# A two-layer decoder trunk on one core: row sums, maximum broadcast, gates and head norm of its mLSTM mixer, done in another way

## The chip, the cores and the metric

The kernel runs on one core of a Trainium2 chip. The engines of the core run side by side and meet through semaphores: PE (TensorE, matrix products, results into PSUM), DVE (VectorE), ACT (ScalarE), POOL (GpSimd), and SP, which issues DMAs. PEld is the loading of the stationary operand, which can overlap PE. The metric is device time in microseconds (us) of one execution. The kernel before was run three times: 999.59 us is the median, 999.35 the lowest, 1000.89 the highest.

## What is computed

A trunk of two layers over 256 tokens of width 1024, in fp32. Each layer has a SwiGLU block, a mixer, a second SwiGLU block and a gated input embedding, each between RMS norms. Layer 0 mixes with an mLSTM in four heads (keys of 128, values of 256), layer 1 with differential attention over keys and values that are shared. The change is in the mLSTM. Cut to what matters:

```python
def step(carry, inp):                       # reference: chunks of 128 tokens
    C, n, m = carry
    b = jnp.cumsum(lf, axis=-1)
    d = b[..., :, None] - b[..., None, :] + li[..., None, :]
    d = jnp.where(causal, d, -jnp.inf)
    inter = b + m[..., None]
    m_t = jnp.maximum(inter, jnp.max(d, axis=-1))
    w = jnp.exp(d - m_t[..., None])
    qk = jnp.einsum('bhtd,bhsd->bhts', qj, kj) * w
    num = jnp.einsum('bhts,bhsv->bhtv', qk, vj) + ...
    den = jnp.sum(qk, axis=-1) + ...
    h = num / jnp.maximum(jnp.abs(den), jnp.exp(-m_t))[..., None]
...
h = mlstm_chunkwise(q, k, v, log_i, log_f)   # log_i, log_f from x @ w_in[:, gates] + b_gates
h = rms_norm(h, head_norm[:, None, :])
return (jax.nn.sigmoid(o) * h) @ w_out
```

So per head and token there is a weighted sum of values (num), the sum of the weights themselves (den), a division, and an RMS norm over the 256 values of the head.

## The kernel before

**Numbers in parts.** A product of the trunk's weights is done as three fast products: each operand is split into a rounded high part and a remainder (`split`: ACT copies into an fp32r tile, DVE subtracts), and `mm3` (L507) adds high·high, high·low and low·high. An fp32r matmul is one pass of PE; a plain fp32 matmul is two rows in the profile. Weight tiles come as 128x2048 into `wraw` buffers, and become `whi` and `wlo`.

**The order is planned.** The program notes every operation first (`Notes.add`). `Notes.play` (L267) then lays them out with a cost model: per engine it takes, among the operations that can start, mostly the one of lowest rank, which is the order of the program text. For PE a change of operand kind adds a penalty; `kind` (L205) calls transposes "t", everything with an fp32r operand "r", and other matmuls by the size of their stationary operand. Plain fp32 matmuls and transposes are held back until their inputs have been there for a margin; those on one PSUM tile go together. Buffers of a pool are given in order of first use: ten `wraw`, eight `att` (128x512), three each of `sg`, `hh` and `hl`, and in PSUM three banks `accI`, four banks `accO`, one bank `tr`. Since `issue` calls all operations from one place, all stand on L433 in the profile, and one tells them apart by tile names.

**The mixer** is `mlstm` (L996), between about 185 and 285 us. The 256 tokens are two blocks of 128, t = 0 and 1.

- *Queries and keys*: per block two 512-wide products, each evacuated by `transposed` (L986): ACT copies with the norm's factor, PE transposes four 128x128 pieces, DVE copies them to `qT` or `kT`. `transposed` also serves the shared keys and the queries of layer 1, those with a factor.
- *Gates*: `pg` (L1035) has the eight gate rows, spread over 36, along partitions and the tokens along columns, in fp32; `pr` (L1036) spreads the norm's factor over 36 rows by a matmul with the identity. ACT copies `pr`, DVE multiplies. Then biases, log-sigmoid (ACT: exp and ln), a cumulative sum and a running maximum M by scans, all on four rows.
- *Values*: `block_pair` (L718), seven products of a Strassen scheme in place of eight, from `forms` of the inputs (`att` buffers). It ends with `use`; here that is `value`, which ACT does.
- *Heads* (`head`, L1067): PE spreads M's row of this head over 128 partitions (`pm`) and makes the scores (`pS`, fp32); DVE makes the argument of the exponential and, after ACT's exp, the weights `pTh`.
- *Outputs* (`outputs`, L1101): per block, PE makes `pd`, the sums of the weights, by matmuls with a column of ones, and `num`, two heads to a bank; DVE, ACT (squares) and POOL (power of −1/2) make the norm's factor, and DVE scales `num` by it into `hn`.
- *Output gate*: a second `block_pair` makes the gate's inputs and calls `opened` (L1156), which calls `outputs` and `gated`; `gated` multiplies and transposes.
- *Output product*: `proj` (L970) for each block, into two `accO` banks, and `post`.

The rank of the second `block_pair`'s last piece, and what hangs on it:

```python
        use(1, 1, z5)                                   # outputs(1)
        times(ax, quarter(1, 4), wt4, True)             # twelve matmuls
        if not end:
            use(1, 0, u2)                               # gated(0, 1)
        use(0, 1, ax)                                   # gated(1, 0), gated(1, 1)
```

and where the banks are asked for:

```python
        num = acc_out()                                 # two accO banks, for block t
        nums = [num[h // 2][:, h % 2 * DV:(h % 2 + 1) * DV] for h in range(HA)]
```

Of the kernel before, what the change touches and what calls it, by code (L numbers as in the profile page):

```python
# [16 lines left out]
P = 128  # L17
D = 1024
# [417 lines left out]
def trunk(nc, a):  # L436
    def T(shape, tag, bufs, dt=F32):
        return nc.tile("sb", shape, tag, bufs, dt)
# [4 lines left out]
    def acc_out():  # L443
        return [PT("accO", 512, 4) for _ in range(2)]
# [4 lines left out]
    def trp():  # L449
        return PT("tr", 512, 1)  # L450
# [4 lines left out]
    def piece():  # L455
        return T([P, 512], "att", ATT)
# [20 lines left out]
    def pair(*shape):  # L477
        b = T([P, 2, *shape], "wraw", NRAW)
        return [b[:, i] for i in range(2)]
# [506 lines left out]
    def transposed(pi, r, dst, t, c=1.0):  # L986
        q = piece()
        nc.scalar.activation(q, pi, AF.Copy, scale=r)
        pv = transpose4(q, 0)
        if c == 1.0:  # L990
            nc.vector.tensor_copy(dst[:, :, t * P:(t + 1) * P], pv)
        else:
            nc.vector.tensor_scalar(dst[:, :, t * P:(t + 1) * P], pv, c, None, op0=ALU.mult)


    def mlstm(l, xts, rs, raws, epilogue):  # L996
# [9 lines left out]
            out=mask_a[:, :P], in_=mask_a[:, :P], compare_op=ALU.is_ge, fill=BIG,  # L1006
            base=0, pattern=[[1, P]], channel_multiplier=-1,
        )
        ones = T([P, S], "sg", NSG)
        nc.gpsimd.memset(ones, 1.0)  # L1010

        wg = T([P, KD, 8], "att", ATT)
        nc.sync.dma_start(wg, a["mlstm_gates"])
# [14 lines left out]
        for t in range(NT):  # L1028
            tc_ = slice(t * P, (t + 1) * P)
            for b in range(2):  # L1030
                pi = acc_in()
                in_block(pi, xts[t], ws[b])
                transposed(pi, rs[t], qkT[b], t)
            for k in range(KD):
                nc.tensor.matmul(pg[:36, tc_], w36[:, k, :], raws[t][:, k, :], start=k == 0, stop=k == KD - 1)  # L1035
            nc.tensor.matmul(pr[:36, tc_], rs[t].to_broadcast([P, 36]), ident, start=True, stop=True)  # L1036
        rb = T([36, S], "att", ATT)
        nc.scalar.activation(rb, pr[:36, :S], AF.Copy)
        g36 = T([36, S], "att", ATT)
        nc.vector.tensor_tensor(g36, pg[:36, :S], rb, op=ALU.mult)  # L1040
        li = T([HA, S], "att", ATT)
        nc.vector.tensor_scalar(li, g36[0:HA, :], bg[:, 0:1], None, op0=ALU.add)
        z = T([HA, S], "att", ATT)
        nc.vector.tensor_copy(z, g36[32:36, :])
        nc.vector.tensor_scalar(z, z, bg[:, 1:2], None, op0=ALU.add)

        en = T([HA, S], "att", ATT)
        nc.vector.scalar_tensor_tensor(en, z, -1.0, z, op0=ALU.mult, op1=ALU.max)
# [4 lines left out]
        B = T([HA, S], "att", ATT)  # L1053
        nc.vector.tensor_tensor_scan(B, ones[:HA, :], z, 0.0, op0=ALU.mult, op1=ALU.add)
        nc.vector.tensor_tensor(li, li, B, op=ALU.subtract)
        M = T([HA, S], "sg", NSG)
        nc.vector.tensor_tensor_scan(M, li, li, -3.0e38, op0=ALU.max, op1=ALU.max)
        nc.vector.tensor_tensor(B, B, M, op=ALU.add)


        v = pair(D)
        pTs = []

        def value(b, t, src):
            nc.scalar.activation(v[t][:, b * 512:(b + 1) * 512], src, AF.Copy, scale=rs[t])

        def head(h):  # L1067
            pm, pS = acc_out()
            nc.tensor.matmul(pm[:, :S], ident[:HA, h:h + 1].to_broadcast([HA, P]), M, start=True, stop=True)
            arg = T([P, 384], "att", ATT)  # L1070
            nc.vector.scalar_tensor_tensor(
                arg[:, :S], pm[:, :S], at[:, h:h + 1], mask_a, op0=ALU.subtract, op1=ALU.max)
# [26 lines left out]
        room = pair(D)  # L1099

        def outputs(t):  # L1101
            num = acc_out()
            pd = trp()
            parts = [(slice(0, P), 0)] if t == 0 else [(slice(P, S), 0), (slice(S, 384), 1)]
            nums = [num[h // 2][:, h % 2 * DV:(h % 2 + 1) * DV] for h in range(HA)]
# [4 lines left out]
            for h in range(HA):  # L1110
                for i, (c, st) in enumerate(parts):
                    nc.tensor.matmul(nums[h], pTs[h][:, c], v[st][:, h * DV:(h + 1) * DV],
                                     start=i == 0, stop=i == len(parts) - 1)
            den = small(4)
            nc.vector.tensor_copy(den, pd[:, 0:4])
            nden = small(4)
            nc.vector.tensor_scalar(nden, den, -1.0, None, op0=ALU.mult)
            ad = small(4)
            nc.vector.tensor_tensor(ad, den, nden, op=ALU.max)
            mx = small(4)  # L1120
            nc.vector.tensor_tensor(mx, ad, enm[:, t * HA:(t + 1) * HA], op=ALU.max)
            c = small(4)
            nc.vector.reciprocal(c, mx)
# [4 lines left out]
            c2 = small(4)  # L1128
            nc.vector.tensor_tensor(c2, c, c, op=ALU.mult)
            vv = small(4)  # L1130
            nc.vector.tensor_tensor(vv, c2, sq, op=ALU.mult)
            ve = small(4)
            nc.vector.tensor_scalar(ve, vv, EPS, None, op0=ALU.add)
            rh = rpow(ve, 4)
            cr = small(4)
            nc.vector.tensor_tensor(cr, c, rh, op=ALU.mult)
            hn = room[t]
            for h in range(HA):
                cc = slice(h * DV, (h + 1) * DV)
# [362 lines left out]
```

## Time and profile before

| what | value |
|---|---|
| median of three runs | 999.59 us |
| span of the profiled execution (the page gives no other time of it) | 998.2 us |
| granted clock of PE, mean | 0.998 |
| mixer, 185 to 285 us: PE busy | 99.67 us |
| mixer: DVE busy | 94.19 us |
| mixer: ACT busy | 72.41 us |
| mixer: POOL busy | 14.06 us |

The profile is one execution, taken by the hardware profiler. Busy time counts an engine's instructions; matmuls are pipelined, so their durations overlap, and the distance between two starts tells what one costs. A row of the timeline has the start, the length, engine, line, operation, the tile written and the tiles read, the shape (for a matmul first the stationary operand's, rows*columns), and how many like it were merged.

### The profile page before, as it was taken

The numbers are of one execution on the slowest core, as the hardware profiler recorded it, in microseconds if no ns is written. First come the engines' busy times: TensorE is split into PE (matmuls) and PEld (weight loads), VectorE is DVE, ScalarE is ACT, GpSimd is POOL, SyncE is SP. The second block draws the span as 40 slices with busy tenths as digits, with TensorE's granted clock in tenths as the row PEclk, the third lists the DMA queues.
The fourth block names the chain that finished last, engine by engine and source line by source line (L and its number), as shares of the span: only waits on it lengthen the run. The fifth ranks groups of instructions, "written<-read, shape, count | busy, mean of one in ns | idle before, by whom it ended". The sixth has DMA issues, their size and how long they took to land.

```text
span 998.2 us, 12473 instructions
## 1 busy us (share of the span) xinstructions
PE 987.7 (99%) x4660; PEld 808.9 (81%) x4660; DVE 869.7 (87%) x897; ACT 688.6 (69%) x914; POOL 86.0 (9%) x122
## 2 busy tenths in 40 slices
PE   8999999999999999999999999999999999999997
PEld 7888888888888888888878888888888888888886
DVE  6977999799999799997799999898984988999883
ACT  7747777568856677776777767686775756776663
POOL 0010000300131000001120000000001200000010
PEclk9999999999999999999999999999999999999999
DMA  9999948766699989674699999964755999895511
GB/s 346 420 339 342 309 176 304 242 207 205 252 345 338 287 298 277 247 284 170 257 298 333 322 355 348 340 227 179 253 211 193 298 305 281 317 262 240 222 66 60
DMA packets 44995, 268.39 MB, mean 269 GB/s; under 512 B 5384, under 2 KB 5768, under 8 KB 16008
## 3 DMA queue, kind: packets, MB, share of 16 engines
q1 hardware_dynamic: 39464, 229.59, 60.0%
q0 software_dynamic: 5184, 37.75, 18.5%
q8 instruction: 36, 0.59, 0.2%
q10 hardware_dynamic: 288, 0.27, 0.1%
q14 instruction: 23, 0.19, 0.1%
HBM read 257.11 MB, written 10.49 MB: 268 GB/s over the span
## 4 chain that ended last, share of the span: by engine, by line
PE 48%; issue 2%; ACT 2%; POOL 1%; DVE 1%; POOLq 0%; DVEq 0%; ACTq 0%
PE accI L433 30%; PE accO L433 15%; PE tr L433 2%; POOL sm L433 1%; ACT sg L433 1%; DVE wlo_0r L433 0%; ACT wraw L433 0%; ACT whi_4r L433 0%; ACT whi_0r L433 0%; ACT att L433 0%; DVE wraw L433 0%; DVE xl_5r L433 0%; DVEq L1498 0%; ACT xh_3r L433 0%; POOLq L1498 0%
## 5 line engine op out<-in xcount | busy, mean ns | idle before, releaser
L433 DVE TENSOR_TENSOR wraw<-wraw,wraw 128x2048 f32<-128x2048 f32 x36 | 82.3, 2285 | 0.2
L433 ACT ACTIVATE whi_2r<-wraw 128x2048 fp32r<-128x2048 f32 (+1 forms) x47 | 75.7, 1619 | 8.8 <-PE accI L433 4.2
L433 ACT ACTIVATE whi_3r<-wraw 128x2048 fp32r<-128x2048 f32 (+1 forms) x46 | 75.6, 1651 | 8.1 <-PE accI L433 3.3
L433 ACT ACTIVATE whi_1r<-wraw 128x2048 fp32r<-128x2048 f32 (+2 forms) x48 | 72.5, 1522 | 12.4 <-PE accI L433 4.0
L433 ACT ACTIVATE whi_0r<-wraw 128x2048 fp32r<-128x2048 f32 (+2 forms) x47 | 72.6, 1550 | 10.2 <-PE accI L433 4.7
L433 ACT ACTIVATE whi_4r<-wraw 128x2048 fp32r<-128x2048 f32 (+1 forms) x45 | 73.5, 1647 | 8.4 <-DVE wraw L433 4.5
L433 ACT ACTIVATE whi_5r<-wraw 128x2048 fp32r<-128x2048 f32 (+1 forms) x47 | 74.0, 1587 | 6.2 <-PE accI L433 4.7
L433 ACT ACTIVATE att<-accI 128x512 f32<-128x512 f32 x72 | 42.9, 596 | 30.2 <-PE accI L433 30.2
L433 POOL DMA_DIRECT2D wraw<-in_ffn_in x32 | 28.5, 891 | 322.0 <-DMA wraw<-in_ffn_in 286.6
L433 POOL TENSOR_SCALAR sm<-sm 128x1 f32<-128x1 f32 x32 | 18.8, 587 | 331.7 <-ACT sg L433 331.7
L433 ACT ACTIVATE sg<-accI,sm 128x256 f32<-128x256 f32 x40 | 18.9, 473 | 32.0 <-PE accI L433 26.9
L433 ACT ACTIVATE sg<-att,sm 128x256 f32<-128x256 f32 x48 | 24.0, 505 | 23.9 <-DVE att L433 23.9
L433 POOL TENSOR_TENSOR sm<-sm,mhalf 128x1 f32<-128x1 f32 (+2 forms) x40 | 30.1, 753 | 113.4 <-DVE sm L433 110.8
L433 ACT ACTIVATE sg<-accO 128x512 bf16<-128x512 f32 (+2 forms) x46 | 20.1, 442 | 22.1 <-PE accO L433 20.0
L433 PEld LDWEIGHTS tr<-ident,sg 128*128 128x128 f32 x176 | 23.0, 140 | 14.4 <-DVE hl_0r L433 2.0
L433 PE MATMUL tr<-ident,sg 128*128 128x128 f32 x176 | 34.1, 275 | 0.0
L433 DVE SCALAR_TENSOR_TENSOR wraw<-wraw,sm,wraw 128x512 f32<-128x512 f32 x32 | 22.6, 749 | 12.3 <-POOL sm L433 12.3
L433 DVE TENSOR_TENSOR att<-accI,att 128x512 f32<-128x512 f32 x36 | 24.7, 687 | 7.7 <-PE accI L433 7.2
L433 DVE SCALAR_TENSOR_TENSOR sg<-accI,sm,sg 128x256 f32<-128x256 f32 x40 | 19.2, 480 | 12.1 <-ACT sg L433 11.9
L433 ACT ACTIVATE att<-accI,sm 128x512 f32<-128x512 f32 (+1 forms) x22 | 14.8, 671 | 20.9 <-PE accI L433 20.9
L433 ACT ACTIVATE sg<-wraw 128x512 bf16<-128x512 f32 x32 | 20.1, 629 | 13.1 <-DVE wraw L433 9.6
L433 DVE SCALAR_TENSOR_TENSOR sg<-att,sm,sg 128x256 f32<-128x256 f32 x48 | 22.9, 481 | 3.4 <-ACT sg L433 3.2
(608 smaller groups left out, 3252.2 us busy)
## 6 DMA issues: line engine op xcount, KB each, us to landing
wraw<-in_ffn_in SPq DMA_DIRECT2D x100, 1024.0 KB, 9.2
wraw<-in_ffn_out SPq DMA_DIRECT2D x44, 1024.0 KB, 7.7
wraw<-in_ffn_in POOLq DMA_DIRECT2D x32, 1024.0 KB, 13.7
wraw<-in_mlstm_in SPq DMA_DIRECT2D x14, 1024.0 KB, 5.1
wraw<-in_ple_gate SPq DMA_DIRECT2D x8, 1024.0 KB, 6.2
wraw<-in_w_kv SPq DMA_DIRECT2D x8, 1024.0 KB, 4.8
home<-wraw SPq DMA_DIRECT2D x28, 256.0 KB, 3.9
wraw<-home SPq DMA_DIRECT2D x14, 512.0 KB, 3.9
```

The lines of the kernel that those rows point to most:

```text
L433: getattr(getattr(self.nc, eng), name)(*args, **kw)
```

## The change

- `transposed`: the second copy, out of PSUM, is ACT's instead of DVE's, with the factor in it.
- Gates: the tokens are along partitions: `raws` is the stationary operand, the 36-wide weights move. ACT scales the result by the norm's factor, PE transposes it into `pr`, and the bias additions read `pr` from PSUM. The separate product, the copy of `z` and the matmul that spread the factor go.
- Maximum: M is held as two fp32r parts, on rows 0 to 3 and 32 to 35 of a tile of 36 rows (`mhl`, an `hh` buffer); `pick` (an `hl` buffer) has the identity's columns twice. `pm` is a single fp32r matmul of the two, with 36 rows. M lies in an `att` buffer instead of an `sg` buffer, and `ones` is four rows instead of 128.
- Values: a `wraw` tile of 2048 columns holds seven heads' values with a column of ones between each pair of heads, the last head's values and its ones lie in an `att` tile. The row sum is the 257th column of the value product. Each head's product has an `accO` bank of its own.
- Norm: |den| and the division are rearranged, so that the factor is (mx²·eps + sq)^(−1/2), without reciprocal and products afterwards.

```diff
-        if c == 1.0:
-            nc.vector.tensor_copy(dst[:, :, t * P:(t + 1) * P], pv)
-        else:
-            nc.vector.tensor_scalar(dst[:, :, t * P:(t + 1) * P], pv, c, None, op0=ALU.mult)
+        nc.scalar.activation(dst[:, :, t * P:(t + 1) * P], pv, AF.Copy, scale=c)
...
-        ones = T([P, S], "sg", NSG)
+        ones = T([HA, S], "sg", NSG)
         nc.gpsimd.memset(ones, 1.0)
+        mhl = T([36, S], "hh", NH, F32R)
+        nc.gpsimd.memset(mhl.bitcast(F32), 0.0)
+        pick = T([36, HA], "hl", NH, F32R)
+        nc.gpsimd.memset(pick.bitcast(F32), 0.0)
+        for i in (0, 32):
+            nc.vector.tensor_copy(pick[i:i + HA, :], ident[i:i + HA, i:i + HA])
...
-                nc.tensor.matmul(pg[:36, tc_], w36[:, k, :], raws[t][:, k, :], start=k == 0, stop=k == KD - 1)
-            nc.tensor.matmul(pr[:36, tc_], rs[t].to_broadcast([P, 36]), ident, start=True, stop=True)
-        rb = T([36, S], "att", ATT)
-        nc.scalar.activation(rb, pr[:36, :S], AF.Copy)
-        g36 = T([36, S], "att", ATT)
-        nc.vector.tensor_tensor(g36, pg[:36, :S], rb, op=ALU.mult)
+                nc.tensor.matmul(pg[:, t * 36:t * 36 + 36], raws[t][:, k, :], w36[:, k, :], start=k == 0, stop=k == KD - 1)
+            g36 = T([P, 36], "att", ATT)
+            nc.scalar.activation(g36, pg[:, t * 36:t * 36 + 36], AF.Copy, scale=rs[t])
+            nc.tensor.transpose(pr[:36, tc_], g36, ident)
...
-        M = T([HA, S], "sg", NSG)
+        M = T([HA, S], "att", ATT)
...
-        v = pair(D)
+        vs, v13 = T([P, 2048], "wraw", NRAW), piece()
+        for i in range(4):
+            nc.gpsimd.memset(vs[:, 513 * i + 256:513 * i + 257], 1.0)
+        nc.gpsimd.memset(v13[:, 0:1], 1.0)
+        nc.scalar.activation(mhl[0:HA, :], M, AF.Copy)
+        nc.vector.tensor_tensor(mhl[32:36, :], M, mhl[0:HA, :].bitcast(F32), op=ALU.subtract)
...
-            nc.scalar.activation(v[t][:, b * 512:(b + 1) * 512], src, AF.Copy, scale=rs[t])
+            if b * t:
+                nc.scalar.activation(vs[:, 1539:1795], src[:, :DV], AF.Copy, scale=rs[t])
+                nc.scalar.activation(v13[:, 1:DV + 1], src[:, DV:], AF.Copy, scale=rs[t])
+            else:
+                c = 1026 * t + 513 * b
+                nc.scalar.activation(vs[:, c:c + 514].rearrange("p (h d) -> p h d", h=2)[:, :, :DV],
+                                     src.rearrange("p (h d) -> p h d", h=2), AF.Copy, scale=rs[t])
...
-            nc.tensor.matmul(pm[:, :S], ident[:HA, h:h + 1].to_broadcast([HA, P]), M, start=True, stop=True)
+            nc.tensor.matmul(pm[:, :S], pick[:, h:h + 1].to_broadcast([36, P]), mhl, start=True, stop=True)
...
-            num = acc_out()
-            pd = trp()
...
+            den = small(4)
+            nums = []
             for h in range(HA):
+                num = PT("accO", 512, 4)
                 for i, (c, st) in enumerate(parts):
-                    nc.tensor.matmul(pd[:, h:h + 1], pTs[h][:, c], ones[:, 0:1],
+                    vc = 1026 * st + 513 * (h // 2) + 256 * (h % 2)
+                    nc.tensor.matmul(num[:, :DV + 1], pTs[h][:, c], v13[:, :DV + 1] if st and h == 3 else vs[:, vc:vc + DV + 1],
                                      start=i == 0, stop=i == len(parts) - 1)
...
+                one = 0 if h % 2 else DV
+                nc.scalar.activation(den[:, h:h + 1], num[:, one:one + 1], AF.Copy)
+                nums.append(num[:, h % 2:h % 2 + DV])
             mx = small(4)
-            nc.vector.tensor_tensor(mx, ad, enm[:, t * HA:(t + 1) * HA], op=ALU.max)
...
+            nc.vector.scalar_tensor_tensor(mx, den, -1.0, den, op0=ALU.mult, op1=ALU.max)
+            nc.vector.tensor_tensor(mx, mx, enm[:, t * HA:(t + 1) * HA], op=ALU.max)
...
+            nc.vector.scalar_tensor_tensor(ve, mx, EPS, mx, op0=ALU.mult, op1=ALU.mult)
+            nc.vector.tensor_tensor(ve, ve, sq, op=ALU.add)
+            cr = rpow(ve, 4)
```

More of the change, by code (lines that the diff above doesn't have):

```diff
@@ L1034, in mlstm @@
             for k in range(KD):
-                nc.tensor.matmul(pg[:36, tc_], w36[:, k, :], raws[t][:, k, :], start=k == 0, stop=k == KD - 1)
-            nc.tensor.matmul(pr[:36, tc_], rs[t].to_broadcast([P, 36]), ident, start=True, stop=True)
-        rb = T([36, S], "att", ATT)
-        nc.scalar.activation(rb, pr[:36, :S], AF.Copy)
-        g36 = T([36, S], "att", ATT)
-        nc.vector.tensor_tensor(g36, pg[:36, :S], rb, op=ALU.mult)
+                nc.tensor.matmul(pg[:, t * 36:t * 36 + 36], raws[t][:, k, :], w36[:, k, :], start=k == 0, stop=k == KD - 1)
+            g36 = T([P, 36], "att", ATT)
+            nc.scalar.activation(g36, pg[:, t * 36:t * 36 + 36], AF.Copy, scale=rs[t])
+            nc.tensor.transpose(pr[:36, tc_], g36, ident)
         li = T([HA, S], "att", ATT)
-        nc.vector.tensor_scalar(li, g36[0:HA, :], bg[:, 0:1], None, op0=ALU.add)
+        nc.vector.tensor_scalar(li, pr[0:HA, :S], bg[:, 0:1], None, op0=ALU.add)
         z = T([HA, S], "att", ATT)
-        nc.vector.tensor_copy(z, g36[32:36, :])
-        nc.vector.tensor_scalar(z, z, bg[:, 1:2], None, op0=ALU.add)
+        nc.vector.tensor_scalar(z, pr[32:36, :S], bg[:, 1:2], None, op0=ALU.add)
         en = T([HA, S], "att", ATT)
@@ L1101, in outputs @@
         def outputs(t):
-            num = acc_out()
-            pd = trp()
             parts = [(slice(0, P), 0)] if t == 0 else [(slice(P, S), 0), (slice(S, 384), 1)]
-            nums = [num[h // 2][:, h % 2 * DV:(h % 2 + 1) * DV] for h in range(HA)]
+            den = small(4)
+            nums = []
             for h in range(HA):
+                num = PT("accO", 512, 4)
                 for i, (c, st) in enumerate(parts):
-                    nc.tensor.matmul(pd[:, h:h + 1], pTs[h][:, c], ones[:, 0:1],
+                    vc = 1026 * st + 513 * (h // 2) + 256 * (h % 2)
+                    nc.tensor.matmul(num[:, :DV + 1], pTs[h][:, c], v13[:, :DV + 1] if st and h == 3 else vs[:, vc:vc + DV + 1],
                                      start=i == 0, stop=i == len(parts) - 1)
[L1110 to L1119, printed above, removed]
+                one = 0 if h % 2 else DV
+                nc.scalar.activation(den[:, h:h + 1], num[:, one:one + 1], AF.Copy)
+                nums.append(num[:, h % 2:h % 2 + DV])
             mx = small(4)
-            nc.vector.tensor_tensor(mx, ad, enm[:, t * HA:(t + 1) * HA], op=ALU.max)
-            c = small(4)
-            nc.vector.reciprocal(c, mx)
+            nc.vector.scalar_tensor_tensor(mx, den, -1.0, den, op0=ALU.mult, op1=ALU.max)
+            nc.vector.tensor_tensor(mx, mx, enm[:, t * HA:(t + 1) * HA], op=ALU.max)
             sq = small(4)
@@ L1127, in outputs @@
                                      accum_out=sq[:, h:h + 1])
[L1128 to L1131, printed above, removed]
             ve = small(4)
[L1133 to L1136, printed above, removed]
+            nc.vector.scalar_tensor_tensor(ve, mx, EPS, mx, op0=ALU.mult, op1=ALU.mult)
+            nc.vector.tensor_tensor(ve, ve, sq, op=ALU.add)
+            cr = rpow(ve, 4)
             hn = room[t]
```

## The prediction, made before the changed kernel was run

> **What bounds the kernel now.** I read the head of the page first: busy time of each engine, then the chain of work that ended last.
>
> ```profile
> span 998.2 us, 12473 instructions
> PE 987.7 (99%) x4660; PEld 808.9 (81%) x4660; DVE 869.7 (87%) x897; ACT 688.6 (69%) x914; POOL 86.0 (9%) x122
> PE 48%; issue 2%; ACT 2%; POOL 1%; DVE 1%; POOLq 0%; DVEq 0%; ACTq 0%
> ```
>
> PE is busy 99% of the span, and of the named part of the chain almost all is PE. So an edit is worth what it takes off PE's row, less what PE then waits for. The busy windows around the mixer (all of it between 185 and 285 us) show how close the others are (columns: PE, PEld, DVE, ACT, POOL busy us with counts, clock, DMA share, GB/s), the list of PE's waits shows how little it waits, and two rows of PE's timeline (start, length, then what) the step from matmul to matmul:
>
> ```profile
> 200.00:214.00 14.00, 14.00 (x82) 11.36 (x80) 12.27 (x7) 8.32 (x6) 0.42 (x1) 1.00 0.43 150
> 214.00:238.00 24.00, 24.00 (x112) 19.24 (x111) 23.06 (x37) 19.30 (x26) 1.40 (x2) 1.00 0.85 246
> 238.00:268.00 30.00, 29.67 (x147) 24.57 (x147) 28.01 (x42) 27.76 (x43) 4.03 (x2) 1.00 0.56 197
> PE tr L433 <- DVE wraw L433: 0.5, 2, 0.3
> 268.12 0.61 PE L433 MATMUL accO<-whi_1r,xh_0r 128*128 128x512 f32 x2
> 268.57 0.62 PE L433 MATMUL accO<-wlo_1r,xh_0r 128*128 128x512 f32 x2
> ```
>
> PE is full, DVE at 88 to 96%, ACT at 59 to 93%. The clock is 1.00, so a PE pass has a fixed price. Since a matmul's duration includes its overlapped tail, I price PE by the distance from one start to the next. Two 512-column fp32r matmuls take 0.45 us that way (268.12 to 268.57), one 0.23.
>
> **Row sums.** The separate sum matmuls of `outputs` (tile `tr`, one column) go. From PE's timeline:
>
> ```profile
> 244.86 0.95 PE L433 MATMUL tr<-sg,att 128*128 128x1 f32 x8
> 245.66 1.97 PE L433 MATMUL accO<-wraw,att 128*128 128x256 f32 x8
> 259.40 1.95 PE L433 MATMUL tr<-sg,att 128*128 128x1 f32 x16
> 261.20 3.70 PE L433 MATMUL accO<-wraw,att 128*128 128x256 f32 x16
> 264.55 0.58 PE L433 MATMUL accI<-whi_0r,xh_4r 128*128 128x512 f32 x1
> ```
>
> An fp32 matmul is two rows (passes). 8 passes take 245.66 − 244.86 = 0.80 us, 16 take 261.20 − 259.40 = 1.80 us: **−2.60 us**. In their place each of the 24 value passes has 257 columns instead of 256: 24 × 0.21/256 = 0.02 us, nothing. Neither group can have been hidden: PE runs on without a gap before and behind it.
>
> **Maximum broadcast.** Each head's `pm` is now an fp32 matmul of four rows:
>
> ```profile
> 223.15 1.47 PE L433 MATMUL accO<-wraw 128*128 128x256 f32 x8
> 224.55 1.12 PE L433 MATMUL accO<-sg,ident 4*128 4x256 f32 x4
> 225.51 0.35 PE L433 MATMUL tr<-ident,att 4*128 4x4 f32 x4
> 225.79 0.50 PE L433 MATMUL accI<-whi_5r,xl_3r 128*128 128x512 f32 x1
> 226.13 0.40 PE L433 MATMUL accI<-whi_5r,xh_3r 128*128 128x512 f32 x1
> 227.98 0.40 PE L433 MATMUL accI<-whi_5r,xl_3r 128*128 128x512 f32 x1
> 228.31 0.69 PE L433 MATMUL accO<-sg,ident 4*128 4x256 f32 x2
> 228.93 0.92 PE L433 MATMUL accO<-wraw 128*128 128x256 f32 x4
> 229.61 0.48 PE L433 MATMUL accI<-whi_2r,xh_5r 128*128 128x512 f32 x1
> 229.92 0.40 PE L433 MATMUL accI<-wlo_1r,xh_5r 128*128 128x512 f32 x1
> ```
>
> Take the visit at 228 us. It begins when the matmul of 227.98 is through (228.21) and ends where the stream is back in step (229.92 − 0.23 = 229.69): 1.48 us. Its four score passes would take 0.70 us alone (8 take 224.55 − 223.15 = 1.40), so one head's broadcast costs 0.78 us: two passes of 0.21, and 0.35 for going to a four-row stationary and back. PE's groups of instructions have eight such passes in all; I take head 3's two, which come in a visit of their own, as of the same form. In the first visit two heads cost (226.13 − 0.23) − 224.55 = 1.35 us, 0.28 of it the small transposes. Together 0.78 + 0.78 + 1.07 = 2.63 us.
>
> Afterwards it is one fp32r pass of 256 columns and 36 rows. Its nearest rows, with 128 rows, take 0.23 us for two; four passes are 0.46 us.
>
> ```profile
> 707.55 0.39 PE L433 MATMUL accI<-whi_3r,xh_3r 128*128 128x512 f32 x1
> 707.87 1.16 PE L433 MATMUL accO<-wraw,wraw 64*128 64x128 f32 x16
> 710.91 0.40 PE L433 MATMUL accO<-hl_0r,hh_0r 128*128 128x256 f32 x2
> 711.14 0.40 PE L433 MATMUL accI<-whi_0r,xh_6r 128*128 128x512 f32 x1
> ```
>
> Whether 36 rows also pay the 0.35 us no row shows. The 64-row stationary pays at its entry what the four-row one does (707.55 to 707.87 is 0.32, 227.98 to 228.31 is 0.33, instead of 0.23), so I take it that they do. The planner's kind calls every fp32r operand alike and will not group the broadcasts; I take three visits, and one more for the small transposes that lose their company: 0.46 + 4 × 0.35 = 1.86, **−0.8 us**. Ends: five visits give −0.4; no visit price but that of the transposes gives −1.8. [...]
>
> **Gates.** The last `pg`, `pr` work of token block 0:
>
> ```profile
> 202.67 0.39 PE L433 MATMUL accI<-whi_1r,xl_4r 128*128 128x512 f32 x1
> 202.99 1.94 PE L433 MATMUL accO<-wraw,att 128*36 128x128 f32 x16
> 204.77 0.38 PE L433 MATMUL accO<-ident,sm 128*36 128x128 f32 x2
> 205.08 0.50 PE L433 MATMUL accI<-whi_1r,xh_4r 128*128 128x512 f32 x1
> 205.41 0.39 PE L433 MATMUL accI<-wlo_3r,xh_4r 128*128 128x512 f32 x1
> ```
>
> From 202.90 to 205.18 it takes 2.28 us. Afterwards 16 passes have 128 stationary and 36 moving columns. One moving column took 1.80/16 = 0.112 us a pass, and 36 can't be cheaper: 1.80 us, with no change of shape. Then a transpose of a 36-column stationary: a pass of 0.11 and 0.35 for going there and back. 1.80 + 0.46 = 2.26: **0**. Ends: were a pass as cheap as those of the 4x4 transposes (0.28/4 = 0.07) both blocks would save 1.3 us; with one more shape change each they lose 0.7. [...]
>
> **What lies beside PE.** `transposed` moves its copies from DVE to ACT: 12 calls (4 here, 4 for the shared keys, 4 for the queries). The norm drops five small DVE operations per block, the gates lose one product and one copy. M's two parts add an ACT copy and a DVE subtraction, the column of ones five memsets on POOL, the row sums eight tiny ACT copies, the split of the last value block one ACT operation. The copies' row:
>
> ```profile
> L433 DVE COPY wraw<-tr 128x512 f32<-128x512 f32 x8 | 5.5, 687 | 0.3 <-PE tr L433 0.2
> ```
>
> DVE loses 12 × 0.69 = 8.3 us, a third of it in the mixer, and the small operations on top; ACT gains about as much. All of it is covered by PE's own work; if that cover failed, the price would be a wait like the 0.3 us of PE's list. DVE has more room than before, so it does not become the bound. I take 0, ends −0.5 (the two waits of that row go) to +0.5 (as many come).
>
> **The banks: the added wait.** `num` takes one `accO` bank per head. There are four. So block 1's four products hold all until the scaling on DVE has read them, and `proj` of block 0 needs two. Before, it used block 0's.
>
> ```profile
> 251.03 3.02 POOL L433 TENSOR_TENSOR sm<-sm,mhalf 128x4 f32<-128x4 f32 x1 [33.35 <-DVE sm L433]
> 254.28 1.66 DVE L433 SCALAR_TENSOR_TENSOR wraw<-accO,sm,wraw 128x256 f32<-128x256 f32 x4
> 266.93 1.01 POOL L433 TENSOR_TENSOR sm<-sm,mhalf 128x4 f32<-128x4 f32 x1 [12.88 <-DVE sm L433]
> 268.17 1.66 DVE L433 SCALAR_TENSOR_TENSOR wraw<-accO,sm,wraw 128x256 f32<-128x256 f32 x4
> ```
>
> Block 1's products end at 264.55, its first scaling (of four in 1.66 us) at 268.17 + 0.42 = 268.6: 4.0 us. PE fills 264.55 to 268.12 = 3.57 us with the last twelve block-pair matmuls and transposes. The scalings come 0.42 apart, so the second bank is free at 4.4. The new chain has fewer small DVE steps between squares and scaling; I allow it 0.4 us: 3.6 and 4.0. I take **+0.4 us**, ends 0 and the rival below. Queued behind the waiting `proj` matmul are only its own followers; all of the next stage waits for them.
>
> **Sum.** −2.60 − 0.8 + 0 + 0 + 0.4 = −3.0 us: span 995.2. The page gives no time around the span; the runs' median, 999.59, is 1.4 above it, and I carry these over: **996.6 us**.
>
> **Rivals.**
> 1. *More is gained* (0.13): 36 rows cost no visit, and the two waits of PE's list go. −2.6 − 1.8 + 0.4 − 0.5 = −4.5: 995.1. For it: the fp32r streams run without a break. Against it: both narrower shapes in the trace pay.
> 2. *The gain is eaten in the first block pair* (0.22). PE went to the heads at 223.15 because `xl_3r` was late:
>
> ```profile
> 224.88 0.67 DVE L433 TENSOR_TENSOR xl_3r<-att,xh_3r 128x512 fp32r<-128x512 f32 x1
> 218.93 2.27 DVE L433 TENSOR_TENSOR wlo_0r<-wraw,whi_3r 128x2048 fp32r<-128x2048 f32 x1
> ```
>
> M and the last value piece now take two of the eight `att` buffers ahead of the Strassen forms. If a form so misses its turn on DVE, it comes one weight split (2.3 us) later, and the shorter broadcast leaves PE less to fill with. −3.0 + 2.3 = −0.7: 998.9. Against it: DVE has four copies (2.7 us) less to do here, and PE has other matmuls.
> 3. *Slower by the banks* (0.08). If the planner puts block 1's products behind the twelve covering matmuls, `proj` waits out the whole chain: 3.6 us as in block 1, or, if POOL's power falls beside a DVE split as in block 0 (3.02 instead of 1.01 us; from the end of its products, 245.66 + 8 × 0.21 = 247.3, to 254.28 + 0.42 = 254.7 is 7.4), 7.0 us. −3.4 + 7.0 = +3.6: 1003.2. It ends slower by over 0.2% from a wait of 5.4 us on. Against it: the products had their inputs long before 259.40, and come ahead in rank.
>
> That the change does not do what it says is in the sum: the gates gain nothing and the broadcast a third.
>
> **How the numbers follow.** Forecast 0.57 (995.4 to 997.5 with the bounds of its terms), rivals 0.13, 0.22, 0.08. The range reaches from a little below rival 1 (half of the gates' favourable end on top) over rival 2 with a bad end: 994.3 to 1000.6; left out are rival 3 and the low tail. A measurement can tell about 0.2%, 2.0 us: faster below 997.6, slower above 1001.6. Faster is the forecast and rival 1, 0.70; same 0.22; slower 0.08.
>
> **What would show it.** The rows `tr<-sg,att` of one column are gone, and PE has 4660 − 24 − 4 − 2 = 4630 matmuls. The broadcast stands as 36*128, 256 columns, four rows, with gaps of some 0.1 us on both sides each time. The gate passes stay at 0.11 us. Between block 1's products and the first `proj` matmul PE waits 0 to 1 us for DVE; a longer wait is rival 3. PE waits near 220 us would be rival 2. If PE's count of passes falls and the span does not, the sum is wrong as a whole: the engine behind PE was the bound.

## The result, and the profile after

Eight runs of each: 1002.54 us after, 999.87 us before, ratio 1.0025 with a 95% interval of 1.0016 to 1.0034. The change costs a quarter of a per cent, where 0.3% were forecast to be gained. The head of the changed kernel's page, and its busy windows of the last two of the three stretches shown before, and of five shorter ones within (columns as there; the granted clock is the first number behind the POOL count):

```profile
span 1001.2 us, 12425 instructions
PE 988.7 (99%) x4630; PEld 808.2 (81%) x4630; DVE 863.0 (86%) x876; ACT 697.4 (70%) x937; POOL 88.7 (9%) x129
...
214.00:238.00 24.00, 21.77 (x80) 15.66 (x79) 20.52 (x32) 18.91 (x23) 1.16 (x2) 0.79 0.82 242
238.00:268.00 30.00, 29.90 (x135) 24.42 (x134) 27.14 (x31) 26.50 (x49) 3.83 (x2) 1.00 0.54 191
...
221.67:225.08 3.41, 2.00 (x10) 1.60 (x11) 3.28 (x8) 3.33 (x4) 0.00 (x0) 1.00 0.99 264
225.08:228.49 3.41, 2.87 (x8) 1.64 (x7) 3.41 (x4) 2.38 (x6) 0.00 (x0) 0.50 1.09 298
228.49:231.91 3.42, 3.35 (x7) 2.12 (x8) 2.96 (x8) 2.03 (x2) 0.00 (x0) 0.50 0.96 316
231.91:235.32 3.41, 3.41 (x9) 2.18 (x8) 2.66 (x3) 2.38 (x3) 0.00 (x0) 0.50 0.45 190
235.32:238.73 3.41, 3.41 (x16) 2.79 (x17) 2.43 (x5) 1.47 (x3) 0.00 (x0) 1.00 0.00 0
```

PE has the 4630 matmuls that were counted, and yet one us more of busy time. The loss lies between 214 and 238 us: PE is idle for 24.00 − 21.77 = 2.23 us there (before: not at all), and runs at a mean clock of 0.79 (before 1.00). The low clock is one stretch from 225.08 to 235.32 us, exactly at one half, so three times 3.41 us long. The missing clock is 24 × 0.21 = 5.0 us of PE time. What PE waited for, and its timeline there:

```profile
PE tr L433 <- DVE att L433: 1.4, 2, 0.9
PE accI L433 <- ACT xh_3r L433: 0.5, 1, 0.5
...
221.07 0.40 PE L433 MATMUL accI<-wlo_4r,xh_1r 128*128 128x512 f32 x1
221.89 0.22 PE L433 MATMUL tr<-ident,att 4*128 4x4 f32 x1 [0.42 <-DVE att L433]
223.05 0.34 PE L433 MATMUL tr<-ident,att 4*128 4x4 f32 x3 [0.94 <-DVE att L433]
223.65 0.50 PE L433 MATMUL accI<-whi_1r,xl_1r 128*128 128x512 f32 x1 [0.26 <-DVE xl_1r L433]
...
226.04 0.63 PE L433 MATMUL accI<-wlo_4r,xh_1r 128*128 128x512 f32 x1
226.47 0.63 PE L433 MATMUL accI<-whi_1r,xl_1r 128*128 128x512 f32 x1
```

From 221.07 to 223.65 PE does one weight pass and four small transposes, and is idle for 0.42 + 0.94 + 0.26 = 1.62 us. The first two waits are for DVE results of the gates, which the transposes need. The product that PE left could not have gone on either: its third operand, the form's low part `xl_1r`, was ready at 222.92 + 0.67 = 223.59. Then the steps between matmuls grow from 0.23 to 0.43 us (226.04 to 226.47). Where the form was held up, in ACT's and DVE's timelines of the changed kernel:

```profile
214.79 1.91 ACT L433 ACTIVATE whi_3r<-wraw 128x2048 fp32r<-128x2048 f32 x1
216.72 1.28 ACT L433 ACT_TABLE_LOAD   x1
...
218.45 1.28 ACT L433 ACT_TABLE_LOAD   x1
...
220.07 0.61 ACT L433 ACTIVATE xh_1r<-att 128x512 fp32r<-128x512 f32 x1
...
215.98 1.27 DVE L433 TENSOR_TENSOR att<-wraw 128x512 f32<-128x512 f32 x2
222.92 0.67 DVE L433 TENSOR_TENSOR xl_1r<-att,xh_1r 128x512 fp32r<-128x512 f32 x1
```

and in the same timelines of the kernel before:

```profile
214.78 0.63 ACT L433 ACTIVATE xh_1r<-att 128x512 fp32r<-128x512 f32 x1
217.27 1.28 ACT L433 ACT_TABLE_LOAD   x1 [1.86 <-DVE att L433]
...
214.07 0.68 DVE L433 TENSOR_TENSOR att<-wraw 128x512 f32<-128x512 f32 x1
217.12 0.67 DVE L433 TENSOR_TENSOR xl_1r<-att,xh_1r 128x512 fp32r<-128x512 f32 x1
```

Before, DVE made the form at 214.07 and ACT rounded it at 214.78, ahead of the table loads of the gates. Now DVE makes it at 215.98, a weight split and two table loads stand ahead of it on ACT, and it is 5.3 us late there; its low part then stands behind the gates' scans on DVE and is 5.8 us late (222.92 for 217.12).

The rows of the parts, again of the changed kernel:

```profile
202.88 1.87 PE L433 MATMUL accO<-att,wraw 128*128 128x36 f32 x16
...
204.90 0.39 PE L433 MATMUL accI<-whi_1r,xh_4r 128*128 128x512 f32 x1
...
205.60 0.27 PE L433 MATMUL accO<-ident,att 128*36 128x128 f32 x1
205.94 0.39 PE L433 MATMUL accI<-wlo_4r,xh_6r 128*128 128x512 f32 x1
...
261.58 3.20 PE L433 MATMUL accO<-wraw,att 128*128 128x257 f32 x14
264.61 0.60 PE L433 MATMUL accO<-att,att 128*128 128x257 f32 x2
264.86 0.58 PE L433 MATMUL accI<-wlo_4r,xh_6r 128*128 128x512 f32 x1
...
270.31 0.62 PE L433 MATMUL accO<-whi_1r,xh_0r 128*128 128x512 f32 x2
```

The gates' 16 passes take (204.90 − 0.23) − 202.88 = 1.79 us, the transpose (205.94 − 0.23) − 205.60 = 0.11: 1.90 instead of 2.28, so 0.8 us less for both blocks. Sixteen value passes with their ones take 264.86 − 261.58 = 3.28 us; without them it was 3.35. From there to `proj` at 270.31 PE runs through: the wait for the banks did not come here.

### The profile page after: what moved, and what is told of

Same layout as the page of the kernel before. It is cut to its first block, busy times and chain, and to the rows that moved or that the text cites. A ratio compares the mean times of both kernels' runs of the same rounds, so it can differ in the third digit from the quotient of the medians.

```text
span 1001.2 us, 12425 instructions
## 1 busy us (share of the span) xinstructions
PE 988.7 (99%) x4630; PEld 808.2 (81%) x4630; DVE 863.0 (86%) x876; ACT 697.4 (70%) x937; POOL 88.7 (9%) x129
## 4 chain that ended last, share of the span: by engine, by line
PE 48%; issue 2%; ACT 1%; POOL 1%; DVE 0%; POOLq 0%; DVEq 0%; ACTq 0%
PE accI L433 31%; PE accO L433 15%; PE tr L433 2%; POOL sm L433 1%; ACT sg L433 0%; ACT whi_4r L433 0%; ACT whi_0r L433 0%; ACT att L433 0%; DVE wraw L433 0%; ACT wraw L433 0%; DVEq L1497 0%; ACT xh_3r L433 0%; POOLq L1497 0%; ACT xh_0r L433 0%; ACT xh_4r L433 0%
## 5 line engine op out<-in xcount | busy, mean ns | idle before, releaser
L433 ACT ACTIVATE hh_0r<-tr 128x256 fp32r<-128x256 f32 x29 | 11.1, 382 | 21.6 <-PE accO L433 14.1
```

The lines of the kernel that those rows point to most:

```text
L433: getattr(getattr(self.nc, eng), name)(*args, **kw)
```

## The experiments

**Where the first wait comes from.** First the copies, back on DVE:

```diff
-        nc.scalar.activation(dst[:, :, t * P:(t + 1) * P], pv, AF.Copy, scale=c)
+        if c == 1.0:
+            nc.vector.tensor_copy(dst[:, :, t * P:(t + 1) * P], pv)
+        else:
+            nc.vector.tensor_scalar(dst[:, :, t * P:(t + 1) * P], pv, c, None, op0=ALU.mult)
```

> The changed kernel with the second copies of transposed back on DVE. In the changed kernel PE waits some 2.5 us between 221 and 224 us because the high part of the first form (xh_1r) is made at 220.07 us, behind two table loads on ACT, instead of 214.78; then the granted clock is 0.5 for about 10 us. Theory A (buffers: M and the last value piece take two att buffers ahead of the forms, so the first form starts late): no great difference, the wait stays, the clock falls below 0.9 somewhere in 220 to 236 us, time 1001 to 1003. Theory B (ACT does the copies and so comes late to the form): the form is split before the table loads, PE waits under 1 us, the clock stays 1.00, time 996 to 998.

Then M back in `sg`, and the last value piece asked for inside `value`, where it is filled:

```diff
-        M = T([HA, S], "att", ATT)
+        M = T([HA, S], "sg", NSG)
...
-        vs, v13 = T([P, 2048], "wraw", NRAW), piece()
+        vs, v13s = T([P, 2048], "wraw", NRAW), []
...
             if b * t:
+                v13s.append(piece())
```

> The changed kernel with M back in an sg buffer and the last value piece asked for only when it is written, behind the forms. Theory A (buffers): the first form is split before the table loads, PE waits under 1 us around 221 us, the clock stays 1.00 there, time 996 to 998. Theory B (copies on ACT): the wait stays, the clock falls, 1001 to 1003.

And both together:

> The changed kernel with both: copies on DVE, M in sg and the late value piece. Both theories: no wait around 221 us, clock 1.00, time 996 to 998. If the time is still over 1000, the cause is in the gates, the broadcast or the row sums themselves.

Measured: copies 1.0024 (1.0015 to 1.0034), buffers 1.0015 (1.0005 to 1.0024), both 0.9996 (0.9986 to 1.0005). The copies alone change nothing, as theory A said. With the buffers the first half of theory A holds: ACT makes `xh_1r` at 211.07 instead of 220.07 us, and the wait at 221 us is gone. The second half, a time of 996 to 998 us, does not: another wait comes at 230. Nor does the kernel with both reach the 996 to 998 us expected of it; by that expectation a loss is left in the gates, the broadcast or the row sums. The copies may still cost something where the buffers are late: 1.0015 and 0.9996 differ, with intervals that touch. PE's and ACT's rows of the second kernel, and its window:

```profile
230.93 0.54 PE L433 MATMUL accI<-whi_2r,xh_5r 128*128 128x512 f32 x1 [1.48 <-ACT att L433]
...
226.99 1.91 ACT L433 ACTIVATE whi_0r<-wraw 128x2048 fp32r<-128x2048 f32 x1 [1.58 <-DMA wraw<-in_mlstm_in]
...
230.29 0.59 ACT L433 ACTIVATE att<-accI 128x512 f32<-128x512 f32 x1
...
230.00:235.00 5.00, 4.07 (x11) 3.25 (x12) 3.45 (x6) 4.12 (x7) 0.00 (x0) 0.66 0.72 300
```

ACT waits 1.58 us for a weight piece; the emptying of PE's bank is queued behind that split. This comes back below. Asking late for the last piece's buffer alone, with M left in `att`:

> The changed kernel with the buffer of the last value piece asked for when it is filled; the running maximum stays in a buffer of the forms, and the copies stay on ACT. Theory (the forms come late because of the number of their buffers taken, each of the two counts): the waits near 221 us become shorter, 1 to 2 us in all in place of 2.5, the low clock behind them lasts one or two stretches of 3.4 us, ratio 1.0010 to 1.0025. Rival (the running maximum alone makes it): the wait stays 2.5 us and the ratio within 0.0005 of 1.0025.

1.0020 (1.0011 to 1.0028), and waits of 0.8, 0.5, 0.2 and 0.2 us for PE between 221 and 225 us. That does not decide. The ratio lies within both ranges, and the waits, 1.65 us in all, are as long as the 1.62 us of the changed kernel, not the 2.5 us that the expectation took for it. Only the low clock behind them is shorter (3.41 us for 10.24), and later waits have come in its place (1.5 us for `wlo_3r`, 1.0 us for `wlo_1r`). So the two buffers together make the form late; what each does alone is not shown.

**Is it the broadcast?** Three runs. In the kernel with both undone, the broadcast's tiles on 128 rows instead of 36 (no change of shape):

```diff
-        mhl = T([36, S], "hh", NH, F32R)
+        mhl = T([P, S], "hh", NH, F32R)
```

> As e3, with the two parts of M and the selector on 128 rows (the rest zero) instead of 36. If a stationary operand of 36 rows costs some 0.35 us for each visit, the broadcast passes now stand in the fp32r stream at 0.11 us each without gaps, and the time is 0.7 to 1.4 us below e3. If it costs nothing: the same as e3 within 0.3 us.

The same kernel, with the planner's margin kept for the narrow fp32r matmul, as it has it for fp32, and with a kind of its own for it:

```diff
-        hold = eng == "tensor" and (name == "transpose" or ins[0].dtype != F32R)
+        hold = eng == "tensor" and (name == "transpose" or ins[0].dtype != F32R or ins[0].ap[0][1] < P)
...
-        if ins[0].dtype == F32R:
+        if ins[0].dtype == F32R and ins[0].ap[0][1] == P:
```

> As e3, and the planner treats the fp32r broadcast as it treated the fp32 one: held back until its inputs have been there for the margin, with a kind of its own. In e3 PE waits 1.2 us before the third broadcast (224.49 to 225.68), for the argument of head 0 on DVE, and the clock then is 0.5 for some 3 us. If the lost margin is the cause, the wait goes, the clock stays above 0.95 in 220 to 240 us, and the time is 1.5 to 3 us below e3 (997 to 998.5). If the plan slips there for another reason, the wait comes at another matmul and the time is that of e3.

And the kernel before with the two-part broadcast alone (`mhl`, `pick` and `pm` of the change):

```diff
-            nc.tensor.matmul(pm[:, :S], ident[:HA, h:h + 1].to_broadcast([HA, P]), M, start=True, stop=True)
+            nc.tensor.matmul(pm[:, :S], pick[:, h:h + 1].to_broadcast([36, P]), mhl, start=True, stop=True)
```

> The kernel before with the broadcast as two fp32r parts alone. By the prediction: -0.8, ends -0.4 and -1.8 (998.2 to 999.6 where before is 1000). If the fp32r broadcast is placed without the margin and PE waits for it, with a falling clock behind: 1000.5 to 1003, and a granted clock of 0.5 somewhere in 222 to 240 us.

Measured: 0.9993 (0.9983 to 1.0002), 1.0033 (1.0020 to 1.0045), 1.0040 (1.0027 to 1.0053). One visit with 36 rows, and with 128, in PE's timelines of the kernels with both undone:

```profile
230.49 0.39 PE L433 MATMUL accI<-wlo_0r,xh_6r 128*128 128x512 f32 x1
230.81 0.38 PE L433 MATMUL accO<-hh_0r,hl_0r 36*128 36x256 f32 x1
231.12 1.57 PE L433 MATMUL accO<-wraw 128*128 128x256 f32 x8
232.45 0.48 PE L433 MATMUL accI<-whi_3r,xl_6r 128*128 128x512 f32 x1
```

```profile
231.03 0.40 PE L433 MATMUL accI<-wlo_0r,xh_6r 128*128 128x512 f32 x1
231.26 0.28 PE L433 MATMUL accO<-hh_0r,hl_0r 128*128 128x256 f32 x1
231.38 1.47 PE L433 MATMUL accO<-wraw 128*128 128x256 f32 x8
232.61 0.47 PE L433 MATMUL accI<-whi_3r,xl_6r 128*128 128x512 f32 x1
```

232.45 − 230.49 = 1.96 us against 232.61 − 231.03 = 1.58: 36 rows cost 0.38 us a visit, as the prediction took it (0.35). But taking this off does not show in the time: 0.2 us by the medians, where 0.7 to 1.4 us were expected if 36 rows cost a visit. Nor does the margin help: the wait below stays, so a lost margin is not its cause, and the time fits neither expectation, since a new wait of 2.5 us for `whi_0r` comes near 264 us. The broadcast alone lost more than its expectation allowed for (4.0 us where 3 was the end), with the wait and the low clock that it named. What stays in all of them is this row of the kernel with both undone, and in the broadcast alone its like with 1.12 us:

```profile
225.68 0.38 PE L433 MATMUL accO<-hh_0r,hl_0r 36*128 36x256 f32 x1 [0.91 <-DVE att L433]
```

The third head's broadcast needs a bank that DVE has yet to read (`att<-accO`, the argument), and the low part `xl_3r` of the next form is not there either. Before, PE was at the longer fp32 broadcasts here. But that they filled the time is only part of it: in the broadcast alone DVE makes `xl_3r` at 226.95 us, behind M's subtraction (224.31) and the arguments of four passes (225.64, 1.39 us), where before it made it at 224.88, ahead of the arguments.

**Row sums alone.** The kernel before with the values and their ones, the late last piece, one bank per head and the short norm:

```diff
-                    nc.tensor.matmul(pd[:, h:h + 1], pTs[h][:, c], ones[:, 0:1],
+                    nc.tensor.matmul(num[:, :DV + 1], pTs[h][:, c], v13s[0][:, :DV + 1] if st and h == 3 else vs[:, vc:vc + DV + 1],
```

> The kernel before with the row sums, the values beside ones (last piece asked for late), a bank for each head and the short norm alone. By the prediction's terms: -2.6 for the sum matmuls, +0.4 for the banks: 997.5 to 998.2 where before is 1000. If the banks are what costs, the first output product waits 2 us or more after the products of block 1 and the time is 1000 or more.

0.9997 (0.9988 to 1.0006), a clock of 1.00 in this stretch, and a span of 998.3 us to 998.2: 2.6 us of passes are gone, and the time is not. Both sides of the expectation miss. PE is now idle for 1.90 us between 200 and 285 us, before for 0.33; these 1.6 us are waits, and the other 1.1 us were not traced. From the list of its waits:

```profile
PE accO L433 <- DVE wraw L433: 1.0, 1, 1.0
PE accI L433 <- DVE wlo_3r L433: 0.7, 1, 0.7
```

The first is the prediction's wait for the banks, the second one for the low part of a weight; both come from DVE.

**What a wait does to the clock.** The kernel before, with a chain of small POOL operations (ten; in the second kernel five, `range(4)`) and one extra transpose that needs it, in the first SwiGLU block, where nothing else is changed:

```diff
+            if (l, f, j, t) == (0, 0, 4, 1):
+                a4 = small(4)
+                nc.gpsimd.tensor_tensor(a4, h[:, :4], h[:, :4], op=ALU.mult)
+                for _ in range(9):
+                    b4 = small(4)
+                    nc.gpsimd.tensor_tensor(b4, a4, mhalf[:, :4], op=ALU.pow)
+                    a4 = b4
+                nc.tensor.transpose(trp()[:4, :P], a4, ident)
```

> The kernel before with a chain of ten small POOL operations in the first SwiGLU block whose end PE waits for by one more transpose (its result isn't used). The planner thinks the chain shorter than it is, so PE waits some 2 to 5 us there, where nothing else is changed. If a wait of PE costs its own length: time up by the wait. If the granted clock falls behind a long wait: it shows 0.5 for some microseconds after it, and the time rises by the wait and 1 to 5 us more.

> Before's kernel with a chain of five small GpSimd operations (ten in the run before) ahead of one extra transposition on PE in the first SwiGLU block. Theory (the granted clock falls behind any wait of PE that leaves a stretch of some 3.4 us too empty): a wait of 1.5 to 2.5 us gives one stretch at a lower clock, and the lag grows to the wait and 0.5 to 2 us more. Rival (it needs a long wait as that of 4.9 us, and the low clock behind the shorter waits of the changed kernel comes of something else in that stretch): the clock stays 1.00 and the lag is the wait alone, within 0.3 us.

1.0077 (1.0061 to 1.0093) and 1.0038 (1.0025 to 1.0052). The waits, and the window of 3.41 us behind them, of the long one and then of the short one:

```profile
98.21 0.27 PE L433 MATMUL tr<-ident,sm 128*4 128x128 f32 x1 [4.72 <-POOL sm L433]
...
98.81:102.22 3.41, 3.41 (x10) 2.67 (x9) 1.96 (x1) 1.54 (x2) 1.12 (x2) 0.50 1.05 389
```

```profile
89.77 0.27 PE L433 MATMUL tr<-ident,sm 128*4 128x128 f32 x1 [2.10 <-POOL sm L433]
...
90.26:93.67 3.41, 3.41 (x10) 2.66 (x9) 0.41 (x1) 0.04 (x1) 0.00 (x0) 0.50 1.02 430
```

The clock is at one half for 3.41 us each time, which takes 1.7 us. So the waits should cost 4.7 + 1.7 = 6.4 and 2.1 + 1.7 = 3.8 us. Between a matmul that stands ahead of both waits and one that stands behind them (at 59.19 and 114.27 us in the kernel before) the two kernels lose 6.6 and 4.1 us. So the theory holds against the rival of the short wait's run. Whether it comes in every execution is not shown: three of the short wait's four runs took 1004.3 to 1005.3 us, the fourth 1001.8. The fourth fits an execution without the low stretch (its mean clock on record is 0.998, that of the three 0.996 and 0.997); it has no profile that would show it.

**Gates alone, gates with row sums, and the broadcast undone in the changed kernel.** The first two are the kernel before with these parts of the change, the third is the changed kernel with the reverse of the broadcast's diff above (M stays in `att`). The gates' core:

```diff
-                nc.tensor.matmul(pg[:36, tc_], w36[:, k, :], raws[t][:, k, :], start=k == 0, stop=k == KD - 1)
+                nc.tensor.matmul(pg[:, t * 36:t * 36 + 36], raws[t][:, k, :], w36[:, k, :], start=k == 0, stop=k == KD - 1)
```

> Before's kernel with the token-major gates alone; the row sums, the broadcast and the copies are before's. Theory (what leaves PE in this stretch only counts where PE doesn't then wait for DVE): the 32 gate passes take 0.11 us as before, the four 36-row passes and their visits go (0.38 us per block of 256 tokens by the row distances of the changed kernel), and the chain on DVE loses four instructions, so that no new wait of PE over 1 us appears and the granted clock stays 1.00: ratio 0.9990 to 1.0000. Rival (the gates, now made by a scaled copy on ACT and a transpose per 128 tokens, come later than before and hold up the first forms): a wait of 1 us or more between 205 and 225 us and a ratio of 1.0010 or more.

> Before's kernel with the row sums, the late last piece of the values, the short head norm and the token-major gates, with before's 32-bit broadcast and before's copies on DVE. Theory (the broadcast's 16 passes are what PE fills with while DVE makes the low parts): the waits near 221 and 225 us are gone, the clock stays 1.00 there, waits of some 0.7 us remain near 250 and 262 us, and the bank wait near 266 us stays about 1 us: ratio 0.9980 to 0.9995, the fastest of all so far. Rival (PE's gain here is always given back to DVE): 0.9997 as the row sums alone, within 0.0005.

> The changed kernel with before's 32-bit broadcast from M; the row sums, the gates, the copies on ACT and M and the last value piece in buffers of the forms stay. Theory (two separate losses: the forms that come late because two of their buffers are taken, and the shorter broadcast): PE still waits 1 us or more near 221 us, the clock falls behind it, and the ratio is 1.0005 to 1.0025, between the kernel before and the changed one. Rival (the broadcast alone is the loss, the buffers cost nothing once PE has its filler): no wait of 1 us near 221 us, clock 1.00, ratio 0.9980 to 0.9995.

1.0030 (1.0018 to 1.0042), 1.0007 (0.9998 to 1.0015), 1.0094 (1.0079 to 1.0110): the first matches its rival in time but not in the wait's place, and the other two miss both sides. The third is the one to note: the changed kernel with the long broadcast back is not better but worse. PE is idle there for 5.95 us of the 75 between 205 and 280 us (2.6 of them for the banks, 1.9 for `xh_3r`, 1.1 ahead of the broadcast), and the clock is at one half for four stretches of 3.41 us. One reason that the runs share stands in the rows of the gates alone; ACT's, PE's, and the window:

```profile
226.61 1.92 ACT L433 ACTIVATE whi_0r<-wraw 128x2048 fp32r<-128x2048 f32 x1 [1.37 <-DMA wraw<-in_mlstm_in]
...
229.91 0.59 ACT L433 ACTIVATE att<-accI 128x512 f32<-128x512 f32 x1
...
230.56 0.50 PE L433 MATMUL accI<-whi_2r,xh_5r 128*128 128x512 f32 x1 [1.10 <-ACT att L433]
...
225.00:230.00 5.00, 4.45 (x22) 3.08 (x20) 3.75 (x6) 3.60 (x5) 0.00 (x0) 1.00 1.02 283
```

and in the same places of the kernel before:

```profile
225.19 1.91 ACT L433 ACTIVATE whi_0r<-wraw 128x2048 fp32r<-128x2048 f32 x1
...
225.00:230.00 5.00, 5.00 (x26) 3.69 (x25) 4.96 (x9) 4.97 (x8) 0.00 (x0) 1.00 0.97 270
```

The DMA share is full in both (1.02 and 0.97). Both orders put this split ahead of the emptying of a bank (`att<-accI`); before, the piece was there by 225.19, here it lands near 226.6, and PE waits behind a transfer. Why it lands later was not traced. The planner prices these transfers at 423 bytes per ns; the last column of the windows, in GB/s, shows 283 and 270. The kernels with the buffers late, with rows and gates, and with the broadcast undone show the same (ACT waits 1.6, 1.4 and 1.9 us for that piece). The test was to tell the planner a lower figure, for these weights alone:

```diff
-                o.lat = size / (270.0 if slow else 423.0) + 100
+                o.lat = size / (270.0 if slow else 340.0 if "mlstm_in" in src.tensor.name else 423.0) + 100
```

in the gates alone, in the changed kernel with both undone, and in the kernel before:

> The token-major gates alone, as in the run of the gates alone, with the bandwidth that the order assumes for the mLSTM's weights lowered from 423 to 340 bytes per ns; the work is the same, only its order changes. Theory (the gates gain 0.7 us of PE, and lose it because the split of a weight piece stands on ACT ahead of the emptying of a PE bank and waits there for its transfer): that split stands behind the emptying, the waits of ACT for a transfer and of PE for the bank near 229 us (1.4 and 1.1 us) are gone, a wait of about 1 us is left near 270 us, ratio 0.9985 to 1.0005. Rival (the loss is in the gates' own steps): the wait near 229 us or one like it stays, ratio 1.0020 to 1.0040 as before.

> The changed kernel with copies and buffers undone, with the same lower bandwidth in the order. Theory (PE is free here and DVE and the weights set the pace, so an order that knows the weights better changes little): the waits near 225 us (1.2 and 0.5 us) stay, the later ones move; ratio 0.9985 to 1.0005. Rival (a better order lets the gains of the three parts through): waits after 240 us under 1 us in all, ratio 0.9975 to 0.9985, faster than both kernels.

> The control: the kernel before with the same lower bandwidth in the order. Theory (before's order has no wait of PE over 0.5 us in this stretch, so there is nothing to win): 1.0000 to 1.0020, with a wait of some 0.8 us near 273 us. Rival (the lower figure is simply the truer one and helps every kernel): 0.9985 to 0.9995.

1.0006 (0.9997 to 1.0015), 1.0005 (0.9996 to 1.0014), 1.0017 (1.0008 to 1.0026). In the gates alone the wait near 229 us is gone. Against the control, which has a like wait of 1.1 us for DVE's `wlo` behind 270 us, they gain 0.85 us by the medians of eleven runs each (1000.94, 1000.46 to 1001.28, for 1001.79, 1001.21 to 1002.61). That is what PE's rows gave them, 0.8. So a saving on PE can come through. Against the kernel before they gain nothing, since the new order costs what they bring. With both undone nothing is won, as the theory said: the waits near 225 us stay, and new ones of 1.0 and 0.8 us come for `wlo_1r`. The control also shows how far an order alone goes: the same work, planned with another figure, takes 0.17% more. Every version here was planned anew, so differences of that size between two versions need not belong to the part that was taken out.

No version beats the kernel before by what can be measured; the best is both undone with 128 rows, 0.9993 (0.9983 to 1.0002).

## Why the prediction was wrong

- **Row sums, −2.60**: right as PE time (the passes are gone, the value passes cost no more), and worth nothing alone: 1.6 us came back as waits for DVE, the rest in a way that was not traced.
- **Broadcast, −0.8**: the visit price was right, 0.38 for the assumed 0.35 us. But time taken off PE is a gain only where PE has something else to do. Alone the broadcast loses 0.4%.
- **Gates, 0**: mis-sized on the good side, −0.8: a pass of 36 columns takes the 0.112 us assumed, but the transpose takes 0.11 us in all, not 0.46. So this transpose with its 36 *columns* paid no visit, and the 36 *rows* did. It is not shown for few columns in general: the gate passes before, of 36 columns too, were entered after 0.32 us (202.67 to 202.99), where a matmul is mostly followed after 0.23.
- **What lies beside PE, 0**: this is the step that failed. "DVE has more room than before, so it does not become the bound" was argued from DVE's sum of busy time, with a wait of 0.3 us as the price if PE's cover failed. DVE did get the room: it was busy for 20.52 us of 214 to 238, before for 23.06. The form was late all the same, because what counts is when each form and low part is ready, and that hung on its buffer and on its place in the orders of ACT and DVE. The price was 2.23 us of idle PE and the low clock. The room to catch up is small: in the kernel before, three things are near their limit together, PE (by the windows from 214 to 268 us busy in 53.67 of 54 us), DVE (51.07 of 54) and, from 210 to 230 us, the transfers (a DMA share of 0.92 to 1.05 in each 5 us). In most of the runs what PE lost there came back as a wait for one of the others.
- **Banks, +0.4**: did not come in the changed kernel, where the late forms left PE 5.45 us of cover (264.86 to 270.31). It came, with 1.0 us, in the row sums alone, with 1.4 in the kernel with the copies on DVE, and with 2.6 in the one with the broadcast undone: the term depends on the order more than its 0 to 0.4 us allowed.
- **"The clock is 1.00, so a PE pass has a fixed price"**: the other failure, and the larger one in us. The price held only while PE was fed: 5.0 us of PE's clock are missing between 214 and 238 us, behind the waits. The sum had no term for it.

**Rival 2** named the place and the first link: M and the last value piece take two `att` buffers, a form misses its turn, and PE waits near 220 us. Its other link, that the shorter broadcast leaves less to fill with, is not borne out: with the long one back, the changed kernel lost 0.94%. It had a chance of 0.22 and a price of 2.3 us. The wait is about as large (2.23 us idle), but the clock behind it more than doubles it. Summed anew: −2.6 − 0.8 − 0.8 for the parts (the broadcast's by the prediction's estimate), +2.0 for idle time between 214 and 268 us (2.23 + 0.10, before 0.33), +4.7 for the clock (5.0 less what falls on idle time in the slow ten us, (0.54 + 0.07) / 2) gives +2.5. PE's last matmul starts 2.6 us later than before (993.24 for 990.67); the spans differ by 3.0, and the other 0.4 us lie behind that matmul.

What stays open: what each of the two buffers does alone; how much of the 0.94% with the broadcast undone belongs to which of its waits; and, since every version was planned anew, how far the loss belongs to this change and how far to an order that happened to suit the kernel before.

## What to carry to other kernels

Before you price a saving on the full engine, look at the other engines and the DMA share in the same stretch; if they are nearly full too (here DVE 95%, the DMA share about 1), the saving may well come back as waits, so try each part of a change alone. Ask of each tile that feeds the full engine when it will be ready, not only how busy its maker is, and count the buffers that a new tile takes from such tiles. Count a new wait of PE not by its length alone: here slow stretches that took 1.7 us each, one to three of them, came behind waits of 0.91 to 4.72 us, and none behind one of 1.5 us. Where an order is planned, plan the old kernel with another figure too: it tells how much an order alone can move.

## What the runs showed of the hardware

The low clock came in portions of 3.41 us at half speed, 1.7 us of deficit each: one behind the waits of 4.72, 2.10 and 1.48 us above (the last is that of the kernel with late buffers, window of 0.66), one behind 0.91 and 0.21 us in the kernel with both undone, three in a row in the changed kernel. In the two executions read for it they start on one grid: with the broadcast undone at 224.54, 231.37 and 275.75 us, which is 2 and 13 times 3.41 us apart; in the changed kernel at 225.08 us and, when PE has almost no work left, at 996.49 us, which is 226 times 3.413 us later. The length of the wait alone does not decide: in the gates with row sums PE waited 1.5 us for `wlo_3r` near 265 us with the clock at 1.00, while 2.1 us was enough in the short wait's run, and so were 0.91 and 0.21 us in the kernel with both undone. Nor was PE idle throughout ahead of a slow portion: in the changed kernel it was busy for 2.00 of the 3.41 us from 221.67 on and for 2.87 of those from 225.08 on, and the next portion was slow both times.

What separates the two cases can be read from the traces, by a count made afterwards that no run was set up to test. Take every portion of the grid, give each pass its step at full clock (0.227 us for 512 columns of fp32r, by 17 steps from 249.75 to 253.61 us in the kernel before, and 0.21 us for 256 of fp32, by 16 passes from 261.20 to 264.55 us there; fewer columns are taken in proportion), and weigh it by the rows of its stationary operand over 128. In the 18 profiles there are 5063 portions between 20 and 980 us. All 19 with 1.30 us of such work or less were followed by one at half speed; all the others had 1.34 us or more and were followed by one at full speed. In the kernel before the lowest has 1.58 us, from 257.84 us on, and the clock stayed at 1.00. In the changed kernel the four portions from 221.67 us on have 1.30, 1.10, 1.25 and 1.69 us; the second to the fourth are the three at half speed. So the count fits the three portions there: in the first two of them PE, at half speed and with idle time and passes of 36 rows in between, did no more than 1.10 and 1.25 us of such work. The portions from 98.81 us in the long wait's run and from 90.26 us in the short one's are full of passes of 128 rows at half speed, 0.43 us apart: by the count 1.8 us each (3.41/0.43 × 0.227), and the clock behind them was 1.00.

The other surprise is the shape: as a transpose between fp32r matmuls, a stationary of 36 columns and 128 rows cost 0.11 us in all, while a visit with one of 36 rows and 128 columns took 0.38 us more than with 128 rows (1.96 for 1.58 us).
